# Two rings of four PSUM banks in place of one ring of eight, in a kernel of four transformer layers

## The chip, the cores and the metric

One core of one Trainium2 chip runs the whole kernel. The metric is the device time of one execution in microseconds (us); lower is better. A program that runs on one core has one span, the time from its first to its last instruction; the time of the execution is a little longer.

## The reference, cut to what matters

The input `x` has 1024 tokens of width 1024 in float32. Two blocks follow one another:

```python
# first block, 2 layers
h = rms_norm(x, norm_w[l]); proj = h @ w_in[l]
a = sliding_window_attention(rope(q), rope(k), v, sinks[l]) * silu(z_attn)  # 8 heads of 64, 2 of keys and values, window 128
b = rms(hgrn2_recurrence(silu(q_h), k_h, i_h, log f)) * silu(g_h)           # 4 heads of 128
x = x + (sigmoid(gate_attn) * (a @ w_up_attn[l]) + sigmoid(gate_hgrn) * (b @ w_up_hgrn[l])) @ w_out[l]
# then rms_norm, and the second block, 2 layers
x = x + (gelu(u) * (tril(W_s) @ layer_norm(gelu(v)) + b_s) * silu(z)) @ a_w_out            # gated layer
k, v = rms_norm(x, g_kv) @ w_kv; q, z = rms_norm(x, g_b) @ w_qz                            # 16 heads of 64
x = x + (chunk_attention(q, k, v, rel_bias) * silu(z)) @ b_w_out                           # chunk of 64 and the 8 before it
return rms_norm(x, g)
```

## The kernel before, in words

**Products.** Activations are kept transposed, in tiles of 128 channels by 512 tokens (a "half" of the sequence), and each operand as two float32r parts, a high and a low one. A product is three matmuls for each tile of the contracted width: high by high, high by low, low by high. `unit` (L261 to L263) gives 128 output channels by 512 tokens in 24 matmuls for a width of 1024; `unit_tok` (L275 to L277) gives 128 tokens by 256 channels, `unit_wide` (L289 to L291) 128 tokens by 512 channels for two token blocks at once. Weights come from HBM by DMAs that SP issues (L219, tiles `raw`, three buffers of 1024 columns), are cast to `wh`, and the rest is subtracted into `wl` (eight buffers each), by whichever of VectorE, ScalarE and GpSimd is planned to be free.

**Everything else on TensorE** is short: means of squares as a product with a constant matrix (L383, L1163 for the first norm, L1027 for the last), transposes of keys and queries (L573, L614), scores, transposed probabilities and outputs of the sliding window (L634, L662), the levels of the recurrence (L681 to L820), a bias of the gated layer (L1234, L1239) and its token mixing (L1294), and in the chunk attention scores (L1424), transposes of the probabilities (L1460) and outputs (L1470). Their operands come from VectorE, ScalarE and GpSimd; these three have all their operations on the helper's line L76, so that tiles tell them apart: `hp` a general tile, `khl` the high and low parts of rotated keys (two buffers), `sP` scores, `pT` transposed probabilities, `xd` and `yd` activations that are put by in HBM.

**Banks.** PSUM has eight banks of 128 x 512 float32 here, and every tile of either kind takes a whole bank: `mm()` (L144, L145) for products, `aux()` (L147, L148) for the rest. Both name the same ring, so the banks go round in the order in which the tiles are asked for: a tile has the bank of the one eight tiles before it, of whichever kind.

**Order.** The program is written as units (a product with what is done to its result) and fibers (the short work, in steps that are interleaved with the units by a count of matmuls). When the program is closed, a scheduler fixes the order of the instructions of each engine for good. It may move an instruction past others on its engine where no data speaks against it; that a tile's slot in its ring is free is one of its conditions. On the chip each engine then runs its list in that order and waits on semaphores for operands and for slots.

Of the kernel before, what the change touches and what calls it, by code (L numbers as in the profile page):

```python
# [9 lines left out]
F32 = mybir.dt.float32  # L10
# [9 lines left out]
P = 128  # L20
H = 512
# [75 lines left out]
class Net:  # L97
# [44 lines left out]
        return self.heap(F32R), self.heap(F32R)  # L142

    def mm(self):  # L144
        return self.ps.tile([P, H], F32, tag="bank", bufs=8, name=self.name("mm"))  # L145

    def aux(self):  # L147
        return self.ps.tile([P, H], F32, tag="bank", bufs=8, name=self.name("aux"))  # L148

    def half_banks(self):  # L150

# [1563 lines left out]
```

## Time and profile before

| | |
|---|---|
| time before, median of 3 runs | 3022.28 us (3022.23 to 3022.83) |
| the profiled execution's own time | 3024.32 us |
| its span | 3022.5 us |
| mean granted clock of TensorE, share of full speed | 0.99 |
| busy: PE (TensorE) | 2927.0 us, 97% |
| busy: DVE (VectorE) | 1678.1 us, 56% |
| busy: ACT (ScalarE) | 1449.5 us, 48% |
| busy: POOL (GpSimd) | 1091.5 us, 36% |

The profile is of one execution. PE is the matmuls of TensorE. A wait is put down to the instruction whose end came last before the waiting one began: "PE aux L383 <- DVE hp" is a matmul of line 383 into an `aux` tile that waited for VectorE to write an `hp` tile. In a timeline a number in brackets is the engine's idle time just before the instruction, "x24" are equal instructions put into one row, and a plain fp32 matmul counts as two. The granted clock is a share of full speed; half of it is the lower level, 1.2 in place of 2.4 GHz.

### The profile page before, as it was taken

The page shows a single profiled execution, that of the slowest core. Times are in us where ns is not written, and L with a number is a line of the kernel's source. Part 1 is how long each engine was busy: PE and PEld are TensorE (multiplying, and loading weights), DVE is VectorE, ACT ScalarE, POOL GpSimd, SP SyncE. Part 2 cuts the span into 40 slices and gives each one's busy share as a digit, 9 for nine tenths or more (in the row PEclk, how much of TensorE's full clock was granted, in tenths as well). Part 3 has the DMA queues.
Part 4 walks back from the last instruction along what each step waited for, and adds up shares of the span by engine and source line. Part 5 has one row for each costly group of instructions (what it writes and reads, how often), then busy time and mean ns, then how long its engine had stood idle before and what let it go on. Part 6 is the DMA issues. An engine that isn't in the chain of part 4 may idle for free.

```text
span 3022.5 us, 43638 instructions
## 1 busy us (share of the span) xinstructions
PE 2927.0 (97%) x16188; PEld 2432.3 (80%) x16188; DVE 1678.1 (56%) x3298; ACT 1449.5 (48%) x2927; POOL 1091.5 (36%) x1174
## 2 busy tenths in 40 slices
PE   6999999999999999999999999999999799999997
PEld 5887887888878888788888878888888688878777
DVE  6556745556556666665666533445344644454566
ACT  4665325642357434475334455334544545564552
POOL 4445333543435433444332233213332322232331
PEclk9999999999999999999999999999999899999999
DMA  3212242122522224212243222533234111111123
GB/s 113 84 63 93 89 147 82 66 70 91 182 70 71 73 84 151 99 70 70 74 151 132 101 92 97 166 103 129 95 116 159 56 38 60 38 59 44 64 98 112
DMA packets 101493, 283.47 MB, mean 94 GB/s; under 512 B 11288, under 2 KB 15512, under 8 KB 101280
## 3 DMA queue, kind: packets, MB, share of 16 engines
q1 hardware_dynamic: 100016, 279.51, 27.3%
q8 instruction: 128, 2.10, 0.3%
q10 hardware_dynamic: 1264, 1.17, 0.1%
q14 instruction: 85, 0.70, 0.1%
HBM read 259.66 MB, written 20.97 MB: 93 GB/s over the span
## 4 chain that ended last, share of the span: by engine, by line
PE 89%; DVE 4%; issue 2%; POOL 2%; DMA 1%; ACT 1%; SPq 0%; DVEq 0%; POOLq 0%; ACTq 0%
PE mm L261 20%; PE mm L262 20%; PE mm L263 20%; PE mm L289 3%; PE mm L290 3%; PE mm L291 3%; DVE hp L76 3%; PE aux L703 2%; PE aux L1470 2%; PE aux L1424 2%; PE mm L275 2%; PE aux L1460 2%; PE mm L276 1%; PE mm L277 1%; PE aux L634 1%
## 5 line engine op out<-in xcount | busy, mean ns | idle before, releaser
L261 PE MATMUL mm<-hp,wh 128*128 128x512 f32 (+1 forms) x2816 | 1118.8, 397 | 0.0
L262 PE MATMUL mm<-hp,wh 128*128 128x512 f32 (+1 forms) x2816 | 1093.2, 388 | 2.0 <-POOL hp L76 2.0
L263 PE MATMUL mm<-hp,wl 128*128 128x512 f32 (+1 forms) x2816 | 1093.7, 388 | 0.0
L76 POOL TENSOR_TENSOR wl<-raw,wh 128x512 fp32r<-128x512 f32 x369 | 491.3, 1334 | 800.7 <-ACT wh L76 690.7
L76 ACT CAST wh<-raw 128x512 fp32r<-128x512 f32 x584 | 360.4, 620 | 692.5 <-PE mm L262 467.1
L76 POOL TENSOR_TENSOR hp<-hp,hp 128x256 f32<-128x256 f32 (+3 forms) x347 | 380.5, 1102 | 680.1 <-DVE hp L76 240.3
L261 PEld LDWEIGHTS mm<-hp,wh 128*128 128x128 f32 x2816 | 530.7, 188 | 114.9 <-issue 11.2
L263 PEld LDWEIGHTS mm<-hp,wl 128*128 128x128 f32 x2816 | 530.0, 188 | 110.9 <-issue 0.2
L262 PEld LDWEIGHTS mm<-hp,wh 128*128 128x128 f32 x2816 | 531.1, 189 | 102.0 <-POOL hp L76 3.3
L76 DVE TENSOR_TENSOR wl<-raw,wh 128x512 fp32r<-128x512 f32 x447 | 358.8, 805 | 231.8 <-ACT wh L76 188.7
L76 DVE TENSOR_TENSOR hp<-hp,hp 128x512 f32<-128x512 f32 (+2 forms) x407 | 296.3, 737 | 154.9 <-ACT hp L76 109.3
L76 ACT ACT_TABLE_LOAD x244 | 313.1, 1283 | 22.9 <-PE mm L263 10.5
L76 DVE TENSOR_TENSOR hp<-mm,hp 128x512 f32<-128x512 f32 (+2 forms) x264 | 166.6, 637 | 161.1 <-ACT hp L76 79.3
L76 ACT ACTIVATE hp<-mm 128x512 f32<-128x512 f32 (+2 forms) x304 | 171.4, 574 | 170.0 <-PE mm L291 78.8
L76 DVE CAST wh<-raw 128x512 fp32r<-128x512 f32 x232 | 118.9, 513 | 186.9 <-PE mm L262 148.9
L76 ACT CAST hp<-hp 128x512 fp32r<-128x512 f32 (+1 forms) x206 | 116.0, 574 | 217.9 <-POOL hp L76 179.8
L76 POOL TENSOR_SCALAR sP<-sP,a2l 128x640 f32<-128x640 f32 (+4 forms) x128 | 89.0, 697 | 284.4 <-DVE a2l L76 176.7
L289 PE MATMUL mm<-wh,hp 128*128 128x512 f32 x480 | 188.1, 392 | 0.0
L290 PE MATMUL mm<-wl,hp 128*128 128x512 f32 x480 | 188.1, 392 | 0.0
L291 PE MATMUL mm<-wh,hp 128*128 128x512 f32 x480 | 187.8, 391 | 0.0
L76 ACT ACTIVATE sP<-sP,a2nm 128x640 f32<-128x640 f32 (+4 forms) x128 | 88.3, 691 | 101.1 <-DVE a2nm L76 101.0
L275 PE MATMUL mm<-wh,hp 128*128 128x256 f32 x448 | 133.7, 298 | 0.0
(186 smaller groups left out, 3406.0 us busy)
## 6 DMA issues: line engine op xcount, KB each, us to landing
raw<-in_w_ch_dram SPq DMA_DIRECT2D x128, 512.0 KB, 3.3
raw<-in_g_uz_dram SPq DMA_DIRECT2D x64, 512.0 KB, 3.3
hp<-xd SPq DMA_DIRECT2D x88, 256.0 KB, 4.2
raw<-in_w_up_dram SPq DMA_DIRECT2D x64, 256.0 KB, 2.7
raw<-in_w_o_dram SPq DMA_DIRECT2D x32, 512.0 KB, 3.3
raw<-in_g_v_dram SPq DMA_DIRECT2D x32, 512.0 KB, 4.0
raw<-in_g_o_dram SPq DMA_DIRECT2D x32, 512.0 KB, 3.8
raw<-in_w_wide_dram SPq DMA_DIRECT2D x28, 512.0 KB, 3.9
```

The costliest lines, as they stand in the source:

```text
L76: self.last = f(*args, **kw)
L261: nc.tensor.matmul(ps, wh[:, c : c + P], rh, start=(k == 0), stop=False)
L262: nc.tensor.matmul(ps, wh[:, c : c + P], rl, start=False, stop=False)
L263: nc.tensor.matmul(ps, wl[:, c : c + P], rh, start=False, stop=(k == nk - 1))
L275: nc.tensor.matmul(ps, lh[:, o : o + P], wh[:, c : c + n], start=(k == 0), stop=False)
L289: nc.tensor.matmul(ps, lh[:, s], wh, start=(k == 0), stop=False)
L290: nc.tensor.matmul(ps, lh[:, s], wl, start=False, stop=False)
L291: nc.tensor.matmul(ps, ll[:, s], wh, start=False, stop=(k == KD - 1))
L703: nc.tensor.matmul(ps[:, s], k[:, s], q[:, s], start=True, stop=True)
L1424: nc.tensor.matmul(ps[:, 0:w], lhs[r, o : o + P], rhs[r, k0 : k0 + w], start=(j == 0), stop=(j == 2))
L1460: nc.tensor.transpose(ps[:, j * P : (j + 1) * P], S[:, (i + j) * P : (i + j + 1) * P], self.ident)
L1470: nc.tensor.matmul(po[e * 64 : e * 64 + 64, 0:P], vv, pts[e][:, i * P : (i + 1) * P], start=(i == 0), stop=(i == nb - 1),)
```

## The change

```diff
     def mm(self):
-        return self.ps.tile([P, H], F32, tag="bank", bufs=8, name=self.name("mm"))
+        return self.ps.tile([P, H], F32, tag="mm", bufs=4, name=self.name("mm"))
 
     def aux(self):
-        return self.ps.tile([P, H], F32, tag="bank", bufs=8, name=self.name("aux"))
+        return self.ps.tile([P, H], F32, tag="aux", bufs=4, name=self.name("aux"))
```

Products now go round four banks of their own, and all other tiles round the other four: a tile has the bank of the tile four before it of its own kind. Instructions and their number stay; the scheduler, which has the slots as a condition, gives another order. On PE 537 lines of some 13,600 differ, on ACT 211, on DVE 176, on POOL 62, on SP 23; nearly all are moves over a few rows. In the rows below, the number behind a tile's name is that of the tile in the program.

At the start of the chunk attention, on PE, the first scores (`aux_20567`, `aux_20568`) stood ahead of the value products `mm_20597` and `mm_20624`. Now:

```order
 L276 MATMUL mm_20624<-wl_20442,hp_20026 128x256
 L277 MATMUL mm_20624<-wh_20441,hp_20027 128x256
+L275 MATMUL mm_20676<-wh_20421,hp_19829 128x256
+L1424 MATMUL aux_20567<-hp_20549,hp_20520 128x256
+L1424 MATMUL aux_20568<-hp_20549,hp_20520 128x256
+L1424 MATMUL aux_20567<-hp_20550,hp_20520 128x256
+L1424 MATMUL aux_20568<-hp_20550,hp_20520 128x256
+L1424 MATMUL aux_20567<-hp_20549,hp_20521 128x256
+L1424 MATMUL aux_20568<-hp_20549,hp_20521 128x256
 L1424 MATMUL aux_20664<-hp_20549,hp_20520 128x256
 L1424 MATMUL aux_20665<-hp_20549,hp_20520 128x256
```

All 48 matmuls of the two value products, and one of the third, are now ahead of the first scores.

In the second layer, on PE, the mean of the norm of the first half (`aux_11297`) stood ahead of the key-value product `mm_11319` of the second half, its second matmul four rows later. Now it is almost behind it:

```order
 L276 MATMUL mm_11319<-wl_11112,hp_11008 128x256
 L277 MATMUL mm_11319<-wh_11111,hp_11009 128x256
+L383 MATMUL aux_11297<-hp_11149,ones_d 128x512
 L275 MATMUL mm_11319<-wh_11111,hp_11013 128x256
 L276 MATMUL mm_11319<-wl_11112,hp_11013 128x256
 L277 MATMUL mm_11319<-wh_11111,hp_11014 128x256
+L383 MATMUL aux_11297<-hp_11150,ones_d 128x512
```

Of that product's 24 matmuls 21 are ahead of the mean's first. At the same place, on ACT, the casts of the keys of the third and fourth block of that half (`khl_11496`, `khl_11501`) stood behind the copies of four query results (`mm_11418`, `mm_11419`) and of ten pieces of transposed keys (`aux_11476`, `aux_11487`). Now:

```order
 L76 ACTIVATE hp_11373<-hp_11300 128x512
 L76 ACTIVATE hp_11379<-hp_11373,eps 128x512
+L76 CAST khl_11496<-hp_11263 128x128 x2
+L76 CAST khl_11501<-hp_11263 128x128 x2
 L76 ACTIVATE hp_11468<-mm_11418 128x256
 L76 ACTIVATE hp_11470<-mm_11418 128x256
```

They are ahead of all of these; on POOL the subtractions that follow them passed two rotations of queries in the same way, and the rotations of the keys of the last blocks passed the subtractions of the first two.

In the sliding window, on PE, the scores (L634) passed part of the next wide product, here in the first layer:

```order
 L614 MATMUL aux_4439<-identr,hp_4381 128x128 x4
-L634 MATMUL aux_4454<-hp_777,hp_4438 128x256 x4
-L634 MATMUL aux_4461<-hp_777,hp_4438 128x256 x4
 L289 MATMUL mm_4489<-wh_4065,hp_3056 128x512
 L290 MATMUL mm_4489<-wl_4066,hp_3056 128x512
 L291 MATMUL mm_4489<-wh_4065,hp_3057 128x512
 L289 MATMUL mm_4490<-wh_4065,hp_3056 128x512
+L634 MATMUL aux_4454<-hp_777,hp_4438 128x256 x4
+L634 MATMUL aux_4461<-hp_777,hp_4438 128x256 x4
```

Four matmuls now stand between the transposes of the queries and their scores.

## Rows read from the trace of the kernel before

**Rows 1.** The page, sections 1 and 5.
```profile
PE 2927.0 (97%) x16188; PEld 2432.3 (80%) x16188; DVE 1678.1 (56%) x3298; ACT 1449.5 (48%) x2927; POOL 1091.5 (36%) x1174
...
L76 ACT ACT_TABLE_LOAD x244 | 313.1, 1283 | 22.9 <-PE mm L263 10.5
```

**Rows 2.** Waits of PE, the whole span: us in total, times, longest us.
```profile
PE aux L1163 <- DVE hp L76: 25.1, 2, 17.4
...
PE aux L383 <- DVE hp L76: 10.2, 5, 4.9
PE aux L573 <- POOL khl L76: 7.6, 5, 3.0
PE aux L634 <- ACT hp L76: 4.4, 11, 0.9
...
PE aux L1239 <- ACT hp L76: 3.1, 4, 1.1
...
PE aux L1460 <- ACT pT L76: 1.2, 1, 1.2
```

**Rows 3.** Windows: stretch, length, busy us by engine, granted clock, DMA.
```profile
1200.00:1250.00 50.00, 40.39 (x204) 34.52 (x203) 35.53 (x59) 24.30 (x67) 22.23 (x40) 0.90 0.32 113
...
2340.00:2400.00 60.00, 42.80 (x261) 35.29 (x261) 36.94 (x77) 34.03 (x89) 24.96 (x24) 0.86 0.17 57
2400.00:2880.00 480.00, 479.91 (x3446) 393.35 (x3445) 231.66 (x817) 252.82 (x641) 132.98 (x177) 1.00 0.15 51
```

**Rows 4.** Timeline of PE, chunk attention's start: start, us, instruction [idle before].
```profile
2363.40 0.58 PE L1424 MATMUL aux<-hp,hp 64*128 64x256 f32 x2 [16.37 <-ACT hp L76]
...
2366.38 0.41 PE L275 MATMUL mm<-wh,hp 128*128 128x256 f32 x1
2366.60 0.41 PE L276 MATMUL mm<-wl,hp 128*128 128x256 f32 x1
...
2371.70 0.28 PE L276 MATMUL mm<-wl,hp 128*128 128x256 f32 x1
2371.82 0.28 PE L277 MATMUL mm<-wh,hp 128*128 128x256 f32 x1
2372.03 0.62 PE L1424 MATMUL aux<-hp,hp 64*128 64x256 f32 x6
```

**Rows 5.** Timeline of PE, the second layer's norm and keys.
```profile
1205.79 0.50 PE L383 MATMUL aux<-hp,ones_d 128*128 128x512 f32 x1 [3.48 <-DVE hp L76]
...
1227.98 0.28 PE L573 MATMUL aux<-identr,khl 128*128 128x128 f32 x1 [2.20 <-ACT khl L76]
1231.29 0.91 PE L573 MATMUL aux<-identr,khl 128*128 128x128 f32 x4 [3.03 <-POOL khl L76]
...
1233.88 0.63 PE L289 MATMUL mm<-wh,hp 128*128 128x512 f32 x1
...
1238.44 0.39 PE L289 MATMUL mm<-wh,hp 128*128 128x512 f32 x1
```

**Rows 6.** Timeline of PE, two products behind a wait of L634.
```profile
470.20 0.40 PE L289 MATMUL mm<-wh,hp 128*128 128x512 f32 x1
470.43 0.40 PE L290 MATMUL mm<-wl,hp 128*128 128x512 f32 x1
```

**Rows 7.** Timeline of PE, the last norm.
```profile
2984.81 0.70 PE L1027 MATMUL aux<-hp,ones_f 128*128 128x256 f32 x2 [2.58 <-DVE hp L76]
```

**Rows 8.** Timeline of PE, scores in the tail.
```profile
2885.71 1.14 PE L1424 MATMUL aux<-hp,hp 64*128 64x384 f32 x12
```

**Rows 9.** Timeline of VectorE, reading those scores.
```profile
2886.54 0.56 DVE L76 CUSTOM_DVE_ANT_0 sP<-aux,bias 128x384 f32<-128x384 f32 x1 [2.29 <-PE aux L1424]
```

**Rows 10.** Timeline of PE, one block to the next in the chunk attention.
```profile
2494.51 1.31 PE L1470 MATMUL aux<-pT,hp 128*64 128x128 f32 x20
2495.75 1.32 PE L1424 MATMUL aux<-hp,hp 64*128 64x256 f32 x12
```

**Rows 11.** Timeline of ScalarE, emptying that output product.
```profile
2495.90 0.27 ACT L76 COPY hp<-aux 128x128 f32<-128x128 f32 x1 [0.91 <-PE aux L1470]
```

## The prediction

> **What bounds the kernel now.** The page comes first: TensorE (PE) is busy 97% of the span [rows 1], so time can only go out of PE's idle 3% or out of stretches in which its clock is low. The waits of PE say where that idle time lies [rows 2]. The reader should see two things: each row names an operand that VectorE, ScalarE or GpSimd still had to make (a norm's sum, a split of keys, a copy of transposed queries), and no row counts more than a few waits or, at most, eleven. A ring of banks that runs dry would stand here as many waits of a product or a score tile for the engine that empties the tile before; there is no such row. So eight banks in one ring did not bind on the chip, and the division as such has nothing to give there. It acts in another way: the order of the instructions on every engine is fixed when the kernel is built, with the bank slots as one condition, and other rings give another order. The windows show where a new order can pay [rows 3]: two stretches of 50 and 60 us have PE busy for 40.39 and 42.80 us at a granted clock of 0.90 and 0.86, against 479.91 of 480 us at 1.00 in the steady part of the chunk attention.
>
> **The change, part by part.** No instruction is added or removed; each term is a move. Gains are negative.
>
> *Start of the chunk attention: -5.2.* PE waits 16.37 us for the first scores (L1424), whose keys ScalarE casts late [rows 4]. In the new order 48 matmuls of two value products (L275 to L277) stand ahead of these scores; their operands and banks were free when the wait began. At full clock such matmuls start 0.12 us apart (2371.70, 2371.82), so 5.8 us of work moves into the wait. Right after the wait they start 0.22 apart (2366.38, 2366.60): the lower clock (1.2 GHz in place of 2.4) will then fall on the scores and the products behind them, as it falls on the value products now, and I take 0.6 off. Ends: 3, where only one of the two products fits (24 x 0.12); and 7, the 8.6 us from 2363.40 to 2372.03 less 1.2 for the scores at the low clock (twice the 0.62 that six take at 2372.03). The copies that empty the two products move on ScalarE too, to just behind the cast of the keys, which has come by then. The scores come no sooner, so their softmax has 5.8 us less work of PE to hide behind; two more value products and part of a query product, over 50 matmuls and 6 us, still stand ahead of its transposes (L1460). I cost that at nothing; were that cover too short, the difference would stand as a new wait at L1460.
>
> *Norm of the second layer's first half, and the keys of its second half: -8.* PE idles 3.48, 2.20 and 3.03 us, and behind each the clock is low: a 512-column matmul takes 0.63 us at 1233.88 and 0.39 only from 1238.44 on [rows 5]. The mean of the norm (L383) moves behind 21 of the 24 matmuls of a key-value product: 2.5 us of the 3.48 fill, and some ten of its matmuls no longer run 0.1 us slower than they need: -3.6. Then the casts of the third and fourth block's keys (khl) move ahead of four copies of queries and ten of keys on ScalarE, and their subtractions ahead of two rotations on GpSimd. The khl tile has two buffers, so these casts still follow the first transposes (L573): a cast and two subtractions per block remain, some 1.7 us in place of 5.2. That is -3.5, and with it half of the low clock behind it (from 1231.29 to 1238.44 some 13 such matmuls lose 0.2 each, 2.6): together -8.4, taken as -8. Ends: -3.6, if the rotated queries come late in their turn and only the first move pays, and -11.3, if all the idle and low clock goes. On SP one weight load passes two stores and another one store, towards PE's side; the weights have their buffers back only as PE uses the old ones, so they move with PE.
>
> *Scores of the sliding window (L634): -4.3.* Eleven waits, 4.4 us in all [rows 2]. The three of 0.90 get four matmuls ahead of them; these start 0.23 apart [rows 6], 0.9 us together. The eight of about 0.21 get one. Work goes in where idle was; 0.1 is left over. *Bias of the gated layer (L1239): -2.9*: four waits, 3.1 us, the longest 1.1 [rows 2]; four matmuls of 0.23 go in front of each.
>
> *Last norm: -4.4.* PE waits 2.58 us for the last square of the first quarter [rows 7], then runs part of a product at the low clock. The sum (L1027) moves behind that product's 24 matmuls and one more, 2.9 us, so the wait is filled; without it the clock need not fall, some 1.8 us. Ends: -2.5 (the wait alone) and -4.5. Behind it stand seven more products, which cover the normalising of that quarter.
>
> *Beginning: -1.5.* PE waits 17.4 us for the second sum of squares (L1163) [rows 2], and 49 matmuls move ahead of it. That would be 5.8 us, but later PE waits for the keys, 4.6 of the 7.6 us in the row of L573 <- POOL (the other 3.03 are those of [rows 5]). These follow from that sum, through VectorE's angles, in front of which four weight splits are now put. So what PE gains first it mostly waits for later. A product of 24 matmuls (2.9 us) is moved ahead of these transposes and fills part. Ends: -5 and +2 (the sum 1.1 us later, the splits another).
>
> *New waits for banks: +2.* I followed the last reader of every bank and its next writer through the trace with the new banks. Nearly all are free in time. In the tail, five tiles would wait 0.3 to 0.8 us: the scores of 2885.71 run on to 2886.85, while VectorE reads the first of them until 2887.10 [rows 8, 9]; with four banks the next score tile and the next transposes stand behind such reads. The new order puts other matmuls there, and a load that SP now issues earlier may take away the wait of 1.2 us at L1460 [rows 2]. Ends: 0 and +5.
>
> Sum: -5.2 - 8 - 4.3 - 2.9 - 4.4 - 1.5 + 2 = -24.3 us. The profiled execution took 3024.32 us, so 3000.0; it lies 2.0 above the median of the runs shown, and the forecast is **2998 us**. A sum of the favourable ends gives about -34 (2988), of the unfavourable ends -9 (3013). A measurement of this kernel tells some 0.2% (6 us) from no change.
>
> **A rule against it.** In the steady chunk attention PE goes from one block's output product to the next block's scores without a gap [rows 10]. The Trainium skill, Perfetto Trace Analysis, says under Matmul Optimizations to use all 8 banks for instruction-level parallelism, and under Optimization Strategy that the same gap coming again and again can mean too little PSUM for the next tile. By it half a ring for scores, transposes and outputs would bring such gaps, and the sum would end above 3022. The trace has no such gap with eight; whether four bring one is the second rival.
>
> **Rivals.**
> 1. *The stalls come back behind.* PE arrives earlier and waits for the same chain: the key rotations, the first softmax, the last quarter. For it: 4.6 us at the start are of that kind, and several rows of [rows 2] follow each other down one chain. Against it: the moved work fills waits whose ends do not move, and what follows the largest is 480 us of almost unbroken PE work [rows 3]. By the unfavourable ends, 3024.3 - 9 - 2 = 3013, and where the last norm also gives back its part, up to 3017.
> 2. *Four auxiliary banks bind in the chunk attention: slower.* In 32 of its 64 blocks the scores are in two pieces, four tiles one behind another, and the second pair starts near 2496.22, in the middle of the row at 2495.75 [rows 10]. With four banks it needs the bank that ScalarE empties from 2495.90 to 2496.17 [rows 11]: some 0.05 us to spare. If ScalarE stands in a table load then (1283 ns, [rows 1]), each such block waits up to 1.28 us: 32 x 1.28 = 41 us, 2998 + 41 = 3039. It is slower than before by what can be measured once the wait is over 0.95 us a block ((24.3 + 6) / 32). Against it: ScalarE was idle 0.91 us before that copy and began 0.08 us after the product's end (2494.51 + 1.31); its order there hardly changes.
> 3. *Nothing that counts.* Banks were never short, and the moves on PE are undone by others' order: 3022.
>
> **Chances.** Forecast 0.74 (its own range 2988 to 3010), rival 1 0.14, rival 2 0.05, rival 3 0.07. Faster by over 0.2% (under 3016): 0.74 and most of rival 1, 0.85; within: 0.10; slower: 0.05. The range takes in the forecast and most of rival 1: 2987 to 3016.
>
> **What would show it.** Right: the wait of L1424 is 5 to 6 us shorter; those of L1239, L634 and L1027 nearly gone; L573 waits at most 2 us behind that norm of the second layer, and the clock of that stretch is above 0.95. Wrong: new rows of L1424 or L1460 waiting dozens of times for ScalarE or VectorE (rival 2), or longer waits at L573 and L614 with the sum of waits unchanged (rival 1).

## The result, and the profile after

The changed kernel takes 2993.31 us (median of 4 runs, 2992.82 to 2995.52), the kernel before in the same comparison 3022.56 us (4 runs): a ratio of 0.9903, 95% interval 0.9886 to 0.9920. It is faster by 29.3 us. The forecast was 2998 us, in a range of 2987 to 3016. The profiled execution took 2993.5 us with a span of 2991.7, that of before 3024.32 with 3022.5: 30.8 us less, and the rest of this section is on these two, where it names no other.

The page first, busy time of the engines; against [rows 1] PE has as much to do as before, and a larger share of a shorter span: its idle time (the span less the busy time) falls from 95.5 to 62.9 us.

```profile
PE 2928.8 (98%) x16188; PEld 2430.3 (81%) x16188; DVE 1680.9 (56%) x3298; ACT 1446.5 (48%) x2927; POOL 1093.3 (37%) x1174
```

The waits of PE, all of the span: us in total, times, longest us. Against [rows 2] the rows of L634, L1239 and of L1460 behind ScalarE are gone, L573 <- POOL has 3.4 us in place of 7.6, and L1027 0.9 in place of the 2.58 of [rows 7]. Two rows of products (L275) are new. The one for ScalarE stands at the beginning, at the first product of the program, which waits for an operand; before, PE waited 17.4 us for VectorE at that place (L1163). The row of L573 for ScalarE (3.1) also stands at the beginning now, not in the second layer.

```profile
PE mm L275 <- DVE hp L76: 9.5, 1, 9.5
PE aux L1163 <- DVE hp L76: 9.0, 2, 8.0
PE aux L383 <- DVE hp L76: 7.9, 6, 4.7
PE mm L275 <- ACT hp L76: 7.2, 1, 7.2
...
PE aux L573 <- POOL khl L76: 3.4, 7, 1.6
...
PE aux L573 <- ACT khl L76: 3.1, 1, 3.1
...
PE aux L1027 <- DVE hp L76: 0.9, 1, 0.9
...
PE aux L1424 <- DVE hp L76: 0.2, 1, 0.2
```

The windows, set so that they hold the same pieces of the program as [rows 3] (columns as there): the norm of the second layer with its keys now takes 38.3 us in place of 50, with 2.0 us idle and the clock at 1.00 in place of 0.90; the start of the chunk attention 54 in place of 60, still with idle time and a clock of 0.87. In 480 us of the steady part PE is busy throughout, as before, but starts 3437 matmuls in place of 3446.

```profile
1194.00:1232.30 38.30, 36.31 (x202) 30.83 (x202) 32.79 (x43) 22.36 (x67) 24.02 (x40) 1.00 0.37 124
2318.00:2372.00 54.00, 43.75 (x263) 36.93 (x262) 35.73 (x77) 33.34 (x89) 25.06 (x24) 0.87 0.19 66
2372.00:2852.00 480.00, 480.00 (x3437) 393.91 (x3435) 230.02 (x814) 251.43 (x640) 132.66 (x177) 1.00 0.15 51
```

Where the 30.8 us went, I read from the ends of products: the last matmul of the same product in either trace, so that each difference is the lead that the changed kernel has there.

| place | product | end before, after (us) | lead | gain here | forecast |
|---|---|---|---|---|---|
| beginning | `mm_1120` | 108.28, 105.52 | 2.8 | 2.8 | 1.5 |
| sliding window, first layer | `mm_8279` | 885.97, 879.76 | 6.2 | 3.5 | |
| norm and keys, second layer | `mm_11539` | 1245.43, 1228.61 | 16.8 | 10.6 | 8 |
| sliding window, second layer | `mm_11891` | 1281.37, 1263.25 | 18.1 | 1.3 | 4.3 with the first layer |
| first products of the gated layer | `mm_14947` | 1615.99, 1598.98 | 17.0 | -1.1 | 0 |
| its bias (L1239) | `mm_16646` | 1848.77, 1827.21 | 21.6 | 4.6 | 2.9 |
| chunk attention, start | `mm_20676` | 2375.71, 2347.75 | 28.0 | 6.4 | 5.2 |
| chunk attention and tail | `mm_27128` | 2925.49, 2898.68 | 26.8 | -1.2 | -2 |
| last norm | `mm_27779` | 2993.25, 2962.12 | 31.1 | 4.3 | 4.4 |

The last 0.3 us of lead are lost to the end of the span. A second trace of the changed kernel (run e8 below, 2996.94 us) gives the same gains within 0.6 us, but for two: 9.0 at the norm and 3.6 at the bias. Three places in the timeline of PE (columns as in [rows 4]). At the start of the chunk attention:

```profile
2330.55 0.28 PE L277 MATMUL mm<-wh,hp 128*128 128x256 f32 x1
...
2340.67 0.58 PE L275 MATMUL mm<-wh,hp 128*128 128x256 f32 x1 [9.48 <-DVE hp L76]
2341.19 1.69 PE L1424 MATMUL aux<-hp,hp 64*128 64x256 f32 x12
```

Against [rows 4] the first scores no longer wait. The two value products are done at 2330.8, and PE now waits 9.48 us at the first matmul of the third. The reader should look for what released it, in the timeline of VectorE:

```profile
2339.93 0.69 DVE L76 SCALAR_TENSOR_TENSOR hp<-mm,hp 128x512 fp32r<-128x512 f32 x1 [1.47 <-ACT hp L76]
```

This reads the query product, the fourth product before the third value product: PE starts 0.05 us after its end. The wait is one for a bank of the products' ring, the only long one in the kernel. At the norm of the second layer, against [rows 5], 1.13 us of the 3.48, 0.26 in place of 2.20 and 0.50 in place of 3.03 are left, and in this trace the clock does not fall:

```profile
1199.93 0.47 PE L383 MATMUL aux<-hp,ones_d 128*128 128x512 f32 x1 [1.13 <-DVE hp L76]
...
1216.57 1.19 PE L573 MATMUL aux<-identr,khl 128*128 128x128 f32 x6 [0.26 <-POOL khl L76]
1218.26 0.28 PE L573 MATMUL aux<-identr,khl 128*128 128x128 f32 x1 [0.50 <-POOL khl L76]
```

In the second trace of the changed kernel the waits there are the same (1.15, 0.26 and 0.50 us), but behind them the clock falls: the 512-column matmuls take 0.63 us, as in [rows 5], from 1219.64 to 1222.63:

```profile
1219.64 0.63 PE L289 MATMUL mm<-wh,hp 128*128 128x512 f32 x1
```

So the low clock at this place differs from run to run. And the last norm's sum, which waited in [rows 7], now stands behind the first matmul of the next product, without a wait before its own first matmuls:

```profile
2958.24 0.28 PE L261 MATMUL mm<-hp,hp 128*128 128x256 f32 x1
2958.36 0.60 PE L1027 MATMUL aux<-hp,ones_f 128*128 128x256 f32 x2
2958.60 0.47 PE L262 MATMUL mm<-hp,hp 128*128 128x256 f32 x1
```

### The profile page after: what moved, and what is told of

Read it like the earlier page. It is cut to its first block, busy times and chain, and to the rows that moved or that the text cites. A ratio compares the mean times of both kernels' runs of the same rounds, so it can differ in the third digit from the quotient of the medians.

```text
span 2991.7 us, 43665 instructions
## 1 busy us (share of the span) xinstructions
PE 2928.8 (98%) x16188; PEld 2430.3 (81%) x16188; DVE 1680.9 (56%) x3298; ACT 1446.5 (48%) x2927; POOL 1093.3 (37%) x1174
## 4 chain that ended last, share of the span: by engine, by line
PE 92%; DVE 4%; issue 2%; POOL 1%; DMA 1%; ACT 1%; SPq 0%; DVEq 0%; POOLq 0%; ACTq 0%
PE mm L261 21%; PE mm L262 21%; PE mm L263 20%; PE mm L291 4%; PE mm L290 3%; PE mm L289 3%; DVE hp L76 3%; PE aux L1424 2%; PE aux L703 2%; PE aux L1470 2%; PE aux L1460 2%; PE mm L275 1%; PE mm L276 1%; PE mm L277 1%; PE aux L634 1%
## 5 line engine op out<-in xcount | busy, mean ns | idle before, releaser
L289 PE MATMUL mm<-wh,hp 128*128 128x512 f32 x480 | 187.8, 391 | 0.0
L275 PE MATMUL mm<-wh,hp 128*128 128x256 f32 x448 | 133.8, 299 | 16.6 <-DVE hp L76 9.5
```

What stands on the lines that cost most here:

```text
L275: nc.tensor.matmul(ps, lh[:, o : o + P], wh[:, c : c + n], start=(k == 0), stop=False)
L289: nc.tensor.matmul(ps, lh[:, s], wh, start=(k == 0), stop=False)
```

## The experiments

My theory: the gain is the order's, and the rings matter in that they allow it; a bank as such gives nothing. First the rival to that, the banks as such. Where a time is compared across runs I use the ratio to the kernel before on the same chip, which took 3025 to 3026 us there.

**The old order with the new banks.** The rings are those of the change (four and four). The edit gives every instruction an edge to the one before it in a stored list, so that each engine has the order of the kernel before:

```diff
         Net(ctx, tc, a, out).run(stop)
+        keep_order(tc)
```

> Two rings of four banks as in the change, but the order of the instructions on all five engines is held to that of the kernel before (an edge from each instruction to the next of its engine, for issue alone). If the gain comes from the order (my theory), this is as slow as before: 3022 us, up to 3 us more for new waits for a bank, 3020 to 3026. If it comes from the banks themselves (products and the rest no longer in each other's way in PSUM), it is as fast as the change: 2990 to 2996.

Measured: 3033.37 us, ratio 1.0023 (1.0014 to 1.0032), slower than before by 7 us, above both ranges that I gave. With old order and new banks nothing is gained, so the gain is the order's. The edges do not hide a gain: the run with one place undone, below, holds its order with the same kind of edges and keeps the gains of the other places. The cost is larger than the 3 us that I gave it. With equal orders the distance of each pair of neighbouring matmuls can be compared in both traces: the four second score tiles of L634 that I had passed over in the sum start 0.61 us later each, and three score tiles in the tail 0.95, 0.92 and 0.76: 5.1 us. The timeline of PE at one of the four, and at two in the tail:

```profile
180.80 0.72 PE L634 MATMUL aux<-hp,hp 128*128 128x256 f32 x4
181.86 0.74 PE L634 MATMUL aux<-hp,hp 128*128 128x256 f32 x4 [0.35 <-DVE hp L76]
182.44 0.40 PE L261 MATMUL mm<-hp,wh 128*128 128x512 f32 x1
```

```profile
2889.32 0.61 PE L1424 MATMUL aux<-hp,hp 64*128 64x256 f32 x5 [0.57 <-ACT hp L76]
...
2898.54 0.61 PE L1424 MATMUL aux<-hp,hp 64*128 64x256 f32 x5 [0.54 <-DVE a2m L76]
```

The four matmuls of the second tile no longer follow the first four; they wait for VectorE to leave the bank. The other 2 us I did not trace to places; in the two traces, whose spans are 10.6 us apart, the low clock covers 70.0 us in place of 63.0.

**One ring, two places moved by hand.** The kernel before, in which the program asks for the tiles later:

```diff
-            self.attn_lane["wait"] = 2 * self.attn_lane["gap"]
+            self.attn_lane["wait"] = 3 * self.attn_lane["gap"]
...
+            while late:
+                late.pop()()
             x = xs[j // 2][:, j % 2, :]
...
-                po = self.aux()[:, :Q]
+                late.append(lambda xk=dict(xs), sq=sq, qs=qs, q=q: close(xk, sq, qs, q))
```

> The kernel before with its one ring of eight, two places moved by hand in the program: the first scores of the chunk attention come three steps later (behind two value products), and the sum of the last norm's first quarter is taken behind the next product. If the order alone makes the gain, these two places give what they give in the trace of the change, 6.4 and 4.3 us: 3012 us, 3008 to 3016, with the wait before L1424 some 6 us shorter and that of L1027 (now L1036) nearly gone. If the division itself is needed, 3022.

Measured: 3017.16 us, ratio 0.9964 (0.9950 to 0.9979), faster than before by 8.8 us. Its waits of PE:

```profile
PE aux L1430 <- ACT hp L76: 10.6, 1, 10.6
...
PE aux L1466 <- ACT pT L76: 2.1, 2, 1.9
```

The first scores (now L1430) wait 10.6 us in place of 16.4, and that of the last norm for VectorE has left the list. The row of the transposes (L1466) is not new: 1.9 us of it stand in the tail (2912.12), where the kernel before has the 1.2 us of L1460 [rows 2]; at the first transposes only 0.2 is left. So the order at two places gives 8.8 us with the eight banks in one ring, against the 10.7 that these places gave in the change.

Why one ring keeps a product from passing can be read from the orders. In the kernel before, the 1298 PSUM tiles are first written on PE in exactly the order in which the program asks for them. In the changed kernel that holds within each ring, but at 30 places products, 39 in all, stand ahead of a tile of the other kind that was asked for before them; the table's places are among them. How much moves is less than the counts given with the change, which take in lines of context: rows taken out and put in are 181 on PE, 74 on ACT, 80 on DVE, 24 on POOL and 6 on SP.

**Other sizes.** `bufs=5` and `bufs=3`, then `bufs=3` and `bufs=5`, in the change:

> Five banks for products, three for everything else. Separate rings of any size let a product pass a waiting tile of the other kind, so by the order theory the gains at all places stay; at the start of the chunk attention a third value product fits into the wait (24 matmuls, 2.9 us more), and the four score tiles of a two-piece block must share three banks, for which the new order puts two products' matmuls between them: 2987 to 2998. If four banks for the rest are just enough (rival 2 of the prediction), each of the 32 two-piece blocks waits for VectorE to read a score tile, 0.5 to 1.0 us: 3005 to 3025.

Measured: 3020.58 us, ratio 0.9981 (0.9972 to 0.9991). My expectation fell; the time is that of the rival, but PE has no row of waits for it. By the ends of products the lead is 21.3 us behind the start of the chunk attention and -3.2 at its last block: 24 us lost in the steady part. The groups of L1424 in that part (columns as in [rows 1]: count, busy us, mean ns), first of the change, then with three banks:

```profile
L1424 PE MATMUL aux<-hp,hp 64*128 64x256 f32 (+2 forms) x492 | 55.9, 347 | 0.0
```

```profile
L1424 PE MATMUL aux<-hp,hp 64*128 64x256 f32 (+2 forms) x504 | 75.5, 354 | 1.1 <-DVE a2m L76 0.9
```

The windows differ by twelve matmuls; over all 576 of them the rows are these, of the kernel before, of the change and of three banks:

```profile
L1424 PE MATMUL aux<-hp,hp 64*128 64x256 f32 (+2 forms) x576 | 64.7, 346 | 16.6 <-ACT hp L76 16.4 <-DVE hp L76 0.3
L1424 PE MATMUL aux<-hp,hp 64*128 64x256 f32 (+2 forms) x576 | 67.9, 350 | 0.2 <-DVE hp L76 0.2
L1424 PE MATMUL aux<-hp,hp 64*128 64x256 f32 (+2 forms) x576 | 88.4, 359 | 1.3 <-DVE a2m L76 0.9 <-DVE hp L76 0.2
```

20 us more for the same matmuls with three banks, and 3.2 more with four than with eight. One block in the timeline of PE shows how, first of the change, then with three banks:

```profile
2646.29 1.33 PE L1424 MATMUL aux<-hp,hp 64*128 64x512 f32 x12
```

```profile
2666.40 1.33 PE L1424 MATMUL aux<-hp,hp 64*128 64x512 f32 x9
2667.66 0.50 PE L261 MATMUL mm<-hp,wh 128*128 128x512 f32 x1
2667.99 0.40 PE L262 MATMUL mm<-hp,wh 128*128 128x512 f32 x1
2668.32 0.61 PE L1424 MATMUL aux<-hp,hp 64*128 64x256 f32 x3
```

In the change the twelve matmuls of four score tiles take 1.33 us. With three banks nine take the same 1.33; the last three come after two matmuls of a product and take 0.61 more. That is the scheduler's order: 14 blocks are split so. In 14 others the twelve stand together, and there the bank does come late, though no idle time shows it:

```profile
2471.32 2.04 PE L1424 MATMUL aux<-hp,hp 64*128 64x256 f32 x12
```

```profile
2472.08 0.42 DVE L76 CUSTOM_DVE_ANT_0 sP<-aux,bias 128x256 f32<-128x256 f32 x1 [2.78 <-PE aux L1424]
```

VectorE has read the first score tile at 2472.50, and the first matmul of the fourth tile, inside PE's row, starts at 2472.57. From their start to the next matmul these fourteen take 2.0 us (the first 2.8), where the 31 of the change take 1.27 in the mean.

> Three banks for products, five for everything else. By the order theory the gains stay but for one value product (2.9 us) that no longer finds a bank in the wait at the start of the chunk attention, and the small waits of the steady chunk attention (1.3 us against before) go: 2993 to 2999. If the number of product banks matters by itself, the products by pairs (L289 to L291), which take two banks at once, wait for their results to be read: over 3005.

Measured: 3004.47 us, ratio 0.9925 (0.9910 to 0.9940), 3000 us against the 3022.56 of before, just over the range of the order theory and under the other. By the ends of products it loses 3.5 us to the change at the start of the chunk attention, as expected one product and somewhat more, and 2.9 at the paired products with which the gated layer begins (5.2, of which 2.3 come back), where waits for VectorE are new (L289):

```profile
PE mm L289 <- DVE hp L76: 3.3, 2, 2.7
```

The small losses of the steady part did go, as expected: the scores (L1424) cost 64.4 us over all, and the lead over the kernel before stays at 19.4 to 19.5 up to a product (`mm_24505`) at which the change has lost 0.8 of its own. But just behind it stands one wait that was not expected, with the low clock after it, and takes 3.3:

```profile
2688.96 0.33 PE L1460 MATMUL aux<-ident,sP 128*128 128x128 f32 x1 [1.93 <-ACT pT L76]
```

Before it ScalarE stood idle for 5.68 us until a weight load landed (2686.45), 3.71 at the same place in the change; whether that belongs to the banks or to this one execution no run here shows.

**One place undone, and the change again beside it.** The stored order is that of the change, but for the norm of the second layer:

> The change, with the order of the kernel before put back at one place only, the norm of the second layer's first half and the keys behind it (on all five engines); everywhere else the order of the change is held. In the trace of the change this place gives 10.6 us. If the gains of the places stand by themselves, this is the change plus 10 to 11 us, a ratio to before of about 0.994, with the waits of 3.5, 2.2 and 3.0 us there as before. If what is gained there is only time that PE would have waited for further on, it is as fast as the change: 0.990.

> The change itself, on the same chip as the three beside it: a ratio to before of 0.990 (0.9886 to 0.992), to compare them with.

Measured: the change 2996.05 us, ratio 0.9899 (0.9884 to 0.9914); with the norm's place undone 3004.40, ratio 0.9926 (0.9910 to 0.9943): 8.4 us between them, somewhat less than expected: in the trace of the change here the clock falls at that place, and by the ends of products the place gives 9.0, in the other run 0.2. The waits of PE have the keys' rows back (L573), and the mean's (L383) larger by 2.5 us than in the change:

```profile
PE aux L383 <- DVE hp L76: 10.4, 6, 4.7
...
PE aux L573 <- POOL khl L76: 6.0, 6, 3.0
PE aux L573 <- ACT khl L76: 5.2, 2, 3.0
```

The gain of one place does not come back as a wait further on.

**The bank that is short.** The change, with two value products in one bank:

```diff
             for t in range(4 * halves[0], 4 * halves[-1] + 4):
-                ps = self.mm()
-                self.unit_tok(ps[:, 0:256], x, w, t, 256)
                 if t % 2 == 0:
+                    ps = self.mm()
+                self.unit_tok(ps[:, (t % 2) * 256 : (t % 2) * 256 + 256], x, w, t, 256)
+                if t % 2:
                     vt[c, t // 2] = self.heap()
-                nc.scalar.copy(out=vt[c, t // 2][:, (t % 2) * 256 : (t % 2) * 256 + 256], in_=ps[:, 0:256])
+                    nc.scalar.copy(out=vt[c, t // 2], in_=ps)
```

> The change, and two value products of the chunk attention share one bank (256 columns each), with one copy for both. In the trace of the change PE still waits 9.5 us at the third value product, and what it waits for is VectorE reading the query product four products before: the ring of four product banks. If that reading is right, all 96 matmuls now stand ahead of the first scores, the wait shrinks by 5.8 us, of which some may come back at the first transposes: 3 to 6 us faster than the change, a ratio to before of 0.988 to 0.9895. If the wait is for an operand, no change: 0.990.

Measured: 2991.51 us, ratio 0.9883 (0.9868 to 0.9897), 4.5 us under the change in the same comparison (the two intervals overlap). The wait of 9.5 us at L275 has left the list, and the first scores (now L1425) wait 4.3:

```profile
PE aux L1425 <- ACT hp L76: 4.3, 1, 4.3
```

So the wait was for the bank. By its median this is the fastest version of the study, by less than these runs make sure.

**Why three banks cost without a wait.** The scores' matmuls use 64 rows of PE each, one head the upper, one the lower. The change, heads one after another:

```diff
-                for j, (lhs, rhs) in enumerate(((qh, kh), (qh, kl), (ql, kh))):
-                    for e, ps in enumerate(pss):
+                for e, ps in enumerate(pss):
+                    for j, (lhs, rhs) in enumerate(((qh, kh), (qh, kl), (ql, kh))):
```

> The change, with the three matmuls of one head's scores one after another and then those of the other head, in place of the two heads in turn. With three banks for the rest the scores (L1424) took 75.5 us in place of 55.9 with hardly a wait. My theory: the two heads' matmuls, 64 rows each, run at the same time when they stand in turn and have their banks together, and the shortage of a bank costs by breaking these pairs. Then breaking all of them costs more than breaking half: L1424 busy 90 to 115 us, the whole 35 to 60 us slower than the change, a ratio to before of 1.002 to 1.010. If the pairs don't matter and only the late bank does, no change: 0.990.

Measured: 2996.66 us, ratio 0.9900 (0.9885 to 0.9915), no change. The group and one block:

```profile
L1424 PE MATMUL aux<-hp,hp 64*128 64x256 f32 (+2 forms) x501 | 57.5, 346 | 0.0
```

```profile
2647.93 1.33 PE L1424 MATMUL aux<-hp,hp 64*128 64x512 f32 x12
```

57.5 us, and still twelve matmuls in about 1.3 us: the theory that the turn makes the pairs fell. In the trace their starts still lie two by two, within 0.01 us. The next one: what counts is that both heads' matmuls stand one behind another, with nothing between. The edit emits the second piece's six matmuls by head, with a step of the program (in the order nine matmuls of a product and often some transposes) between the heads:

```diff
+                order = [(j, e) for j in range(3) for e in range(2)]
+                if i:
+                    order.sort(key=lambda t: t[1])
...
+                    if i and (j, e) == (0, 1):
+                        yield
```

> The change (four and four banks), with the scores of the second piece split on purpose: the three matmuls of one head, then nine matmuls of a product, then the three of the other head. Breaking the turn alone cost nothing (L1424 57.5 us, and the six matmuls still began two by two). My theory now: the 64-row matmuls of the two heads run at the same time when both are in PE's queue one behind another, whatever their turn, and with three banks the last tile came too late for that. Then the split costs here what it cost there, without any want of banks: L1424 (now L1429) 72 to 80 us in place of 55.9, the whole 15 to 22 us slower than the change, a ratio to before of 0.995 to 0.9975. If the loss with three banks came from something else, L1429 stays below 62 us and the ratio at 0.990 to 0.992.

Measured: 3026.31 us, ratio 1.0004 (0.9994 to 1.0013). The group and one block:

```profile
L1429 PE MATMUL aux<-hp,hp 64*128 64x256 f32 (+2 forms) x501 | 76.7, 350 | 0.9 <-ACT pT L76 0.8
```

```profile
2664.02 1.33 PE L1429 MATMUL aux<-hp,hp 64*128 64x512 f32 x9
...
2667.86 0.61 PE L1429 MATMUL aux<-hp,hp 64*128 64x256 f32 x3
```

The scores cost 76.7 us as expected, with four banks and nothing short: nine in 1.33 us and three in 0.61, as with three banks. The whole is some 31 us slower than the change, more than the 15 to 22; the other 10 us I did not trace. The step moved transposes too (42 times scores start directly behind one, never in the change), so the run tests the scores' row, not the whole time.

## Why the prediction was right, point by point

- *Eight banks in one ring did not bind, and the change acts through the order.* Right, and shown: new banks with the old order are slower than before, the old ring with two moves is faster. The reading behind it was too weak, though: a ring that runs dry need not stand as a row of waits, as three banks show. What bears it out is the busy time of the scores, 64.7 us with one ring of eight and 64.4 with five banks of their own.
- *Start of the chunk attention, -5.2.* 6.4. The 5.8 us of the two value products, of which I had taken 0.6 off, came out whole, and one matmul of the third value product went along. What the prediction did not see is what is late next: not the transposes but the third value product, for a bank.
- *Norm and keys, -8.* 10.6 in the two traces, 9.0 with the second trace of the change, 8.4 by the undone place. Two steps were too small. The keys' waits, which I left at 1.7 us, came to 0.8. And of the low clock behind them I left half: in one trace of the change nothing of it is left, in the other eight matmuls still run at it. So 8 is nearer to one run than to the other by luck.
- *Scores of the sliding window, -4.3.* 3.5 and 1.3, together 4.8.
- *Bias of the gated layer, -2.9.* 4.6. Behind the first of these waits the clock fell in the trace of before; eight matmuls of the product there start 0.2 us closer together now. I had priced the waits alone. In the second trace of the change the gain is 3.6. Against that 1.1 us are lost just before.
- *Last norm, -4.4.* 4.3.
- *Beginning, -1.5.* 2.8. There the chain took back most of what PE gained first: `mm_299` ends 10.1 us sooner, `mm_823` 2.4.
- *New waits for banks, +2.* 1.2 net in chunk attention and tail, but not where I looked. The steady part loses 2.1, without a wait: the scores' row grows by 3.2 us. The tail gives back 0.9. In the old order the waits cost 5.1, the unfavourable end; the new order puts matmuls into them.
- *Rival 2.* It did not come, but its place was the right one: with three banks the two-piece blocks lose 24 us. Of its mechanism the bank that comes late was right, in half of these blocks; the rest was wrong: VectorE holds the bank, not ScalarE, the other half is the order, and the loss is not a row of waits. Of the rule in the Trainium skill, Perfetto Trace Analysis (Matmul Optimizations), that all 8 banks be used: the kernel with rings of four is faster by 1%, and with five and three, all 8 in use as well, the gain is nearly gone. What decides here is how the tiles share them.

The sum of the terms was -24.3, the traces give -30.8; 2.6 of the difference are the norm's, 1.7 the bias's, 1.3 the beginning's, 1.2 the chunk attention's. The favourable ends add up to -35.0, not to -34.

## What to carry to other kernels

Where a scheduler orders the instructions, one ring for several kinds of tiles also fixes the order among the kinds; a tile that waits for a slow operand then holds back products that wait for nothing. A ring for each kind, or asking for the tile later, lets them pass, and the place to look for it is a long wait of PE with ready products just behind. Then count banks for the tiles that must be open together: here four scores, and at one place six products (with five banks for products PE still waits 7.9 us there, at the fourth value product).

## What the runs showed of the hardware that I had not expected

Two matmuls of 64 rows each, on different halves of PE's rows, run at the same time when they stand one behind another in its order, in either of the turns tried: twelve of them in 1.33 us, in the blocks shown their starts two by two within 0.02 us. When three come later by themselves, they start 0.12 apart or more and take 0.61 us for what was free. Over the steady part this is 55.9 us against 75.5 and 76.7. A bank too few can cost in this way without any wait in the profile, through the order or by coming late; the busy time of the same group of instructions in two runs shows it.
